# First loads of a two-layer decoder kernel: small tables issued ahead of the input, over two DMA queues

## The chip, the cores and the metric

The kernel runs on one core of one Trainium2 chip. The metric is the device time of one execution in microseconds (us), from its first to its last instruction with what the launch adds around it; lower is better. The kernel before takes 354.22 us (median of three runs).

## The reference, cut to what matters

A decoder of two layers works on an input `x` of 256 positions by 1024 features, all in float32. The first layer is an RWKV-7 time mixing, the second a block-sparse attention. What matters here is only how the first layer begins:

```
h  = x * rsqrt(mean(x*x) + 1e-6) * norm_a          # RMS norm, one row per position
xx = shift_by_one_position(h) - h
out_i = (h + xx * mu[i]) @ w_in[:, columns of i]    # i = 0..5: r, decay, k, v, rate, gate
```

`norm_a` is one vector of 1024 numbers, `mu` six of them, `w_in` a 1024 x 4224 matrix. Everything else in the two layers comes after these products.

## The kernel before, in words

The 256 positions are two blocks b of 128 (the partitions of a tile) and the 1024 features two halves n of 512, so x is four tiles of 128 x 512, called here x(n,b): `xb[n, b]`, 256 KB each. They are loaded by four DMAs on the queue of SyncE (SP).

For one block, `norm_row(b)` (line 689) lets ScalarE (ACT) square the two halves and sum each (tile `sq`, lines 691 to 693), VectorE (DVE) add the two sums (tile `rs`, line 695) and GpSimd (POOL) take the power -0.5 (`rsqrt`, line 524). `block(b)` (line 721) then waits for the event "vT" and starts `normed(b, q, r)` (line 699) for both halves q: DVE multiplies x by the row's factor (tile `xn`, line 704), TensorE (PE) transposes it by an identity matrix (line 706), and the transposed tile is multiplied by `norm_a` on its way from PSUM into `hT` (on DVE for q = 0, line 708; on ACT for q = 1, line 712). DVE then forms the difference `xxT` (line 718). From hT and xxT come the mixed inputs `u`, their high and low parts `zhi` and `zlo`, and the first matrix products.

The vectors `norm_a` (8 rows of 128) and `mu` (48 rows of 128) are loaded as one tile `vrow` of 56 rows, transposed by PE (`start`, line 739, and `columns`, line 727) and copied by DVE into `vT`, so that each feature's factor lies on its partition. The identity is the first 128 columns of the table `con`, 64 KB in 128 rows of 512 bytes.

The order of the work on each engine is not written by hand. The kernel is a set of generators; a small planner in Python, the class `Weave` (line 100), walks through them at build time with an estimated cost for every operation, and emits the instructions of each engine in the order in which its own clock reaches them. An engine then runs its instructions strictly in that order on the chip. DMAs are a lane "D" of the planner (`dma`, line 422); all of them go to SP's queue. The first ones are issued by `fetch` (line 495) with the most urgent priority of the loads at the start, -3, in this order: x(0,0), x(1,0), identity, norm weights, mu, x(0,1), x(1,1), two loads of `wl` (the narrow columns of `w_in`), and then the first weight quarter `raw`.

`warm_up` (line 1626) fills PE from the start with matrix products on a tile of zeros, `ps<-zero` in the profile, until the planner's clock says 9.16; they stand in PE's fixed order between the transposes of the start. ACT begins with a table load and one activation `warm` (line 489) that needs that table.

The helper at line 308 records all of DVE's, ACT's and POOL's operations, line 424 the DMAs, line 413 the matrix products and line 417 the transposes, so in the rows these are told apart by their tiles.

Of the kernel before, what the change touches and what calls it, by code (L numbers as in the profile page):

```python
# [12 lines left out]
AF = mybir.ActivationFunctionType  # L13
# [3 lines left out]
P = 128  # L17
T = 256
NB = 2
D = 1024  # L20
# [79 lines left out]
class Weave:  # L100
# [18 lines left out]
    def spawn(self, gen, prio):  # L119

        end, last, fresh = Event(), [None], [0.0]
        self.parts += 1

        def resume(value=None, waited=False):
            if waited:
                fresh[0] = self.now + LAT
            while True:
                try:
                    w = gen.send(value)
                except StopIteration:  # L130
                    self.parts -= 1
                    self.fire(end)
                    return
                value = None
                if isinstance(w, (Op, list)):
                    ops = [w] if isinstance(w, Op) else w
                    left = [len(ops)]

                    def through(op):
                        left[0] -= 1  # L140
                        if not left[0]:
                            last[0] = op.eng if len(ops) == 1 else None
                            resume()
                    for op in ops:
                        self.submit(op, prio, last[0], fresh[0], through)
                    if ops:
                        return
                elif isinstance(w, Event):
                    if w.done is None:
                        w.waiters.append(resume)  # L150
                        return
                    fresh[0] = max(fresh[0], w.done + LAT)
                elif isinstance(w, (Slots, tuple)):
                    slots, n = w if isinstance(w, tuple) else (w, 0)
                    if len(slots.places) < max(n, 1) or slots.waiters and (not slots.urgent or slots.waiters[0][0] <= prio):
                        slots.wait(prio, resume, n)
                        return
                    fresh[0] = max(fresh[0], slots.since + LAT)
                    value = slots.take(n)
                else:  # L160
                    self.at(self.now + w, resume)
                    return
        self.at(self.now, resume)
        return end
# [196 lines left out]
def yoco(ctx, tc, consts, x, norm_a, mu_a, w_in_a, w0_a, w2_a, a0_a, a2_a, kk_a, ka_a, rk_a,  # L361
         gn_w_a, gn_b_a, w_out_a, norm_kv, w_kv, k_norm, norm_b, w_in_b, q_norm_b, w_out_b, out):
    nc = tc.nc
    x2, out2 = x[0], out[0]
# [9 lines left out]
    spawn = weave.spawn  # L374
# [7 lines left out]
    def T_(tag, name, shape=(P, 512), dt=F32):  # L382

        return up.tile(list(shape), dt, name=nm(name), tag=tag, bufs=1)

    def keep(shape, name):
        return cp.tile(list(shape), F32, name=nm(name))
# [34 lines left out]
    def dma(*pairs):  # L422
        us = sum(max(0.475, math.prod(a.shape) * 4 / 260e3 * (2 if a.shape[-1] < 128 else 1)) for a, _ in pairs)
        return Op("D", us, lambda: [nc.sync.dma_start(a, b) for a, b in pairs])
# [43 lines left out]
    def hs(n):  # L468
        return slice(n * 512, (n + 1) * 512)
# [9 lines left out]
    def event(key):  # L479
        return ev.setdefault(key, Event())  # L480

    def fire(key):
        weave.fire(event(key))


    half = keep((P, 8), "half")
    nc.gpsimd.memset(half, -0.5)
    warm = keep((P, 1), "warm")
    nc.scalar.activation(warm, half[:, 0:1], AF.Tanh)
    con = keep((P, C_TRI), "con")  # L490
    xb = {(n, b): T_(f"kk{n}{b}", "x") for n, b in HB}
    vrow, vrow2 = T_("tmp", "vrow", (56, P)), T_("z1", "vrow", (16, P))
    wl = T_("ab", "wl", (P, KT, 2, 64))

    def fetch(key, *pairs):
        yield dma(*pairs)
        fire(key)

    def fetch_first(b):
        for n in range(2):  # L500
            spawn(fetch(f"x{n}{b}", (xb[n, b], x2[b * P:(b + 1) * P, hs(n)])), -3)
    fetch_first(0)
    spawn(fetch("ident", (con[:, 0:128], consts[0:P, 0:128])), -3)
    spawn(fetch("vrow", (vrow[0:8], norm_a[0].rearrange("(a p) -> a p", p=P)),
                (vrow[8:56], mu_a[0].rearrange("i (a p) -> (i a) p", p=P))), -3)
    fetch_first(1)
    spawn(fetch("wl", *((wl[:, :, i, :], w_in_a[0, :, c:c + 64].rearrange("(a p) f -> p a f", p=P))
                        for i, c in enumerate((1024, 3136)))), -3)
# [8 lines left out]
    ident = con[:, C_ID:C_ID + 128]  # L517
# [843 lines left out]
    for i, label in enumerate(ORDER_A):  # L1361
        key, n = label[0], int(label[1])
# [242 lines left out]
    for i, label in enumerate(ORDER_B):  # L1605
        key, n = label[0], int(label[1])
# [152 lines left out]
```

## Time and profile before

| what | value |
|---|---|
| time, median of 3 runs (lowest to highest) | 354.22 us (353.51 to 354.46) |
| the profiled execution's own time | 354.56 us |
| its span, first to last instruction | 352.7 us |
| PE busy | 342.2 us, 97% of the span |
| DVE busy | 286.6 us, 81% |
| ACT busy | 211.1 us, 60% |
| DMA moved | 51.44 MB, mean 146 GB/s |
| mean granted TensorE clock | 0.995 of full speed |

The span is what one profiled execution shows, instruction by instruction; the time of the same execution lies 1.86 us above it. Shares are means over the whole span: the start, of which the change is a part, is some 20 us of it and has limits of its own. A row of a timeline gives the start, the length, the engine, the line, the operation and the tiles, written before and read after the arrow, and in brackets how long the engine had been idle and who ended that.

### The profile page before, as it was taken

To read this page: it belongs to the slowest core of one execution; us is meant where nothing else is said; L and a number is where in the kernel's file an instruction comes from. 1 tells how busy PE (TensorE), PEld (TensorE's weight loads), DVE (VectorE), ACT (ScalarE), POOL (GpSimd) and SP (SyncE) were. 2 spreads that over 40 slices of the span, in tenths; PEclk is the share of its full clock that TensorE was granted. 3 is DMA by queue.
4 is the path that set the end of the run, shared out by engine and by line. 5 is a ranking of instruction groups with operands and counts; after the bars stand their busy time and mean duration, and the time that the engine had idled before them with its cause. 6 is when DMAs were issued, how large, how long until landed. Compare 5 with 4: busy or idle time off the path is not lost.

```text
span 352.7 us, 7611 instructions
## 1 busy us (share of the span) xinstructions
PE 342.2 (97%) x3006; PEld 266.1 (75%) x3006; DVE 286.6 (81%) x572; ACT 211.1 (60%) x415; POOL 46.7 (13%) x71
## 2 busy tenths in 40 slices
PE   8798999999999999999999999999999999999995
PEld 8774877778466775568777788788888878889784
DVE  2899789999999869959769989648868987769823
ACT  5379986754247852265673556645578775688620
POOL 1200050000310000200220522005504005000000
PEclk9899999999999999999999999999999999999999
DMA  7674762673254912356535512565540266503603
GB/s 197 179 205 137 240 192 77 171 215 94 89 151 125 239 59 61 91 134 233 189 111 180 187 60 73 198 222 185 175 164 2 77 228 223 190 1 122 205 35 119
DMA packets 29740, 51.44 MB, mean 146 GB/s; under 512 B 4412, under 2 KB 5764, under 8 KB 29704
## 3 DMA queue, kind: packets, MB, share of 16 engines
q1 hardware_dynamic: 29704, 50.94, 47.4%
q8 instruction: 24, 0.39, 0.5%
q14 instruction: 12, 0.10, 0.1%
HBM read 48.31 MB, written 1.05 MB: 140 GB/s over the span
## 4 chain that ended last, share of the span: by engine, by line
PE 82%; DVE 13%; DMA 1%; issue 1%; POOL 0%; ACT 0%; SPq 0%; DVEq 0%
PE acc L413 56%; PE ps L413 19%; PE ps L417 6%; DVE u L308 3%; DVE wlo L308 2%; DVE zlo L308 1%; DMA tri<-in_consts_dram 1%; DVE z L308 1%; DVE k L308 1%; DVE x L308 1%; DVE xxT L308 1%; DVE tmp L308 1%; DVE kkh L308 1%; DVE XF L308 0%; POOL rs L308 0%
## 5 line engine op out<-in xcount | busy, mean ns | idle before, releaser
L308 DVE TENSOR_TENSOR wlo<-raw,whi 128x1024 fp32r<-128x1024 f32 x70 | 85.4, 1222 | 25.2 <-ACT whi L308 25.0
L308 ACT ACTIVATE whi<-raw 128x1024 fp32r<-128x1024 f32 x70 | 74.1, 1064 | 39.4 <-PE acc L413 23.7
L413 PE MATMUL acc<-wlo,zhi 128*128 128x512 f32 x120 | 51.6, 430 | 1.0 <-DVE wlo L308 1.0
L413 PE MATMUL acc<-whi,zlo 128*128 128x512 f32 x120 | 47.1, 393 | 0.6 <-DVE zlo L308 0.6
L413 PE MATMUL acc<-whi,zhi 128*128 128x512 f32 x120 | 47.1, 392 | 0.0
L413 PE MATMUL acc<-whi,z 128*128 128x512 f32 x128 | 39.8, 392 | 0.0
L413 PEld LDWEIGHTS acc<-wlo,zhi 128*128 128x128 f32 x120 | 22.5, 188 | 7.3 <-DVE wlo L308 1.4
L413 PEld LDWEIGHTS acc<-whi,z 128*128 128x128 f32 x128 | 24.1, 188 | 4.9
L413 PEld LDWEIGHTS acc<-whi,zhi 128*128 128x128 f32 x120 | 22.5, 188 | 5.0
L413 PEld LDWEIGHTS acc<-whi,zlo 128*128 128x128 f32 x120 | 22.6, 189 | 4.8 <-DVE zlo L308 0.9
L413 PE MATMUL acc<-wlo,z 128*128 128x512 f32 x64 | 26.0, 406 | 0.0
L413 PE MATMUL acc<-zb,whi 128*128 128x256 f32 x128 | 23.3, 282 | 0.0
L413 PE MATMUL acc<-whi,zb 128*128 128x512 f32 x64 | 20.0, 394 | 0.0
L413 PE MATMUL acc<-whi,zf 128*128 128x512 f32 x64 | 19.8, 390 | 0.0
L413 PEld LDWEIGHTS acc<-zb,whi 128*128 128x128 f32 x128 | 19.7, 189 | 0.1
L413 PE MATMUL acc<-zb,wlo 128*128 128x256 f32 x64 | 18.9, 295 | 0.0
L308 POOL TENSOR_TENSOR nrm<-nrm,half 128x8 f32<-128x8 f32 x4 | 8.1, 2021 | 78.0 <-DVE nrm L308 78.0
L413 PE MATMUL acc<-raw,zlo 128*128 128x512 f32 x32 | 15.5, 605 | 0.0
L413 PE MATMUL acc<-raw,zhi 128*128 128x512 f32 x32 | 15.0, 606 | 0.0
L413 PEld LDWEIGHTS acc<-wlo,z 128*128 128x128 f32 x64 | 12.1, 189 | 2.9 <-issue 0.5
L413 PEld LDWEIGHTS acc<-whi,zb 128*128 128x128 f32 x64 | 12.1, 189 | 2.6
L308 ACT ACTIVATE zhi<-u 128x256 fp32r<-128x256 f32 (+1 forms) x16 | 7.9, 522 | 10.1 <-DVE u L308 7.0
(215 smaller groups left out, 721.6 us busy)
## 6 DMA issues: line engine op xcount, KB each, us to landing
raw<-in_w_in_a_dram SPq DMA_DIRECT2D x32, 512.0 KB, 4.3
raw<-in_w_kv_dram SPq DMA_DIRECT2D x16, 512.0 KB, 3.7
raw<-in_w_in_b_dram SPq DMA_DIRECT2D x16, 512.0 KB, 4.2
raw<-in_w_out_a_dram SPq DMA_DIRECT2D x8, 512.0 KB, 4.9
raw<-in_w_out_b_dram SPq DMA_DIRECT2D x8, 512.0 KB, 4.5
x<-in_x_dram SPq DMA_DIRECT2D x8, 256.0 KB, 4.4
out_dram<-x SPq DMA_DIRECT2D x8, 128.0 KB, 1.9
NBK<-kkh SPq DMA_DIRECT2D x6, 128.0 KB, 5.8
```

The lines of the kernel that those rows point to most:

```text
L308: op = Op(eng, us, lambda: getattr(obj, name)(*a, **k), table=table, banks=banks(*a, *k.values()), port=port(eng, name, us, a, k))
L413: return us, lambda: nc.tensor.matmul(dst, l, r, **kw), size(r) * (1 if l.dtype == F32R else 4) * min(l.shape[0], size(l)) / P, banks(dst) ...
L417: return max(0.045, 0.1085 * src.shape[0] / P), lambda: nc.tensor.transpose(dst, src, idt), 256 * src.shape[0] / P, banks(dst), src.shape[ ...
```

## The change

The loads of mu, of the norm weights and of the identity are written out ahead of the planner's work. Mu goes to SP's queue as its first DMA; the norm weights, the identity and the tile x(1,0) go, in that order, to ACT's own queue, ahead of the activation `warm`. The other three tiles of x stay on SP's queue, behind mu. In the planner the load of x(1,0) keeps its place and its cost and emits nothing, and one empty operation of the lane D, with the cost of the three small loads (0.475 us each), takes the place of these and then fires both of their events; so the planner's clock, and with it the order of all other instructions, is meant to stay as it was.

```diff
     half = keep((P, 8), "half")
     nc.gpsimd.memset(half, -0.5)
     warm = keep((P, 1), "warm")
-    nc.scalar.activation(warm, half[:, 0:1], AF.Tanh)
     con = keep((P, C_TRI), "con")
     xb = {(n, b): T_(f"kk{n}{b}", "x") for n, b in HB}
     vrow, vrow2 = T_("tmp", "vrow", (56, P)), T_("z1", "vrow", (16, P))
     wl = T_("ab", "wl", (P, KT, 2, 64))
 
-    def fetch(key, *pairs):
-        yield dma(*pairs)
+
+    nc.sync.dma_start(vrow[8:56], mu_a[0].rearrange("i (a p) -> (i a) p", p=P))
+    for a, b in ((vrow[0:8], norm_a[0].rearrange("(a p) -> a p", p=P)), (con[:, 0:128], consts[0:P, 0:128]),
+                 (xb[1, 0], x2[0:P, 512:1024])):
+        nc.scalar.dma_start(a, b)
+    nc.scalar.activation(warm, half[:, 0:1], AF.Tanh)
+
+    def fetch(key, *pairs, issued=False):
+        op = dma(*pairs)
+        if issued:
+            op.emit = lambda: None
+        yield op
         fire(key)
 
     def fetch_first(b):
         for n in range(2):
-            spawn(fetch(f"x{n}{b}", (xb[n, b], x2[b * P:(b + 1) * P, hs(n)])), -3)
+            spawn(fetch(f"x{n}{b}", (xb[n, b], x2[b * P:(b + 1) * P, hs(n)]), issued=(n, b) == (1, 0)), -3)
     fetch_first(0)
-    spawn(fetch("ident", (con[:, 0:128], consts[0:P, 0:128])), -3)
-    spawn(fetch("vrow", (vrow[0:8], norm_a[0].rearrange("(a p) -> a p", p=P)),
-                (vrow[8:56], mu_a[0].rearrange("i (a p) -> (i a) p", p=P))), -3)
+    def small():
+        yield Op("D", 0.475 * 3, lambda: None)
+        fire("ident")
+        fire("vrow")
+    spawn(small(), -3)
     fetch_first(1)
```

## Rows read from the trace of the kernel before

**Rows 1.** The page: its span and the busy time of TensorE.

```profile
span 352.7 us, 7611 instructions
PE 342.2 (97%) x3006; PEld 266.1 (75%) x3006; DVE 286.6 (81%) x572; ACT 211.1 (60%) x415; POOL 46.7 (13%) x71
```

**Rows 2.** The chain that ended last, 0 to 40 us: start, length, what.

```profile
1.04 4.82 PE ps L413 x22
...
6.06 1.09 PE ps L413 x8
...
7.62 0.70 DVE hT L308
...
11.87 4.31 PE ps L413 x24
```

**Rows 3.** Timeline of SP's queue, the first DMA issues.

```profile
0.72 0.86 SPq L424 DMA_DIRECT2D x<-in_x_dram  x2
1.63 0.42 SPq L424 DMA_DIRECT2D con<-in_consts_dram  x1
2.09 0.38 SPq L424 DMA_DIRECT2D vrow<-in_norm_a_dram  x1
2.51 0.32 SPq L424 DMA_DIRECT2D vrow<-in_mu_a_dram  x1
2.87 0.90 SPq L424 DMA_DIRECT2D x<-in_x_dram  x2
```

**Rows 4.** Timeline of ACT, 0 to 8 us.

```profile
0.72 1.28 ACT L489 ACT_TABLE_LOAD   x1 [0.72 <-PEq L1748]
2.01 0.20 ACT L489 ACTIVATE warm<-half 128x1 f32<-128x1 f32 x1
3.39 0.63 ACT L308 ACTIVATE sq<-x 128x512 f32<-128x512 f32 x1 [1.18 <-DMA x<-in_x_dram]
...
4.25 0.63 ACT L308 ACTIVATE sq<-x 128x512 f32<-128x512 f32 x1
...
6.37 0.63 ACT L308 ACTIVATE sq<-x 128x512 f32<-128x512 f32 x1 [1.39 <-DMA x<-in_x_dram]
...
7.07 0.63 ACT L308 ACTIVATE sq<-x 128x512 f32<-128x512 f32 x1
```

**Rows 5.** Timeline of DVE, 5 to 12 us.

```profile
5.01 0.16 DVE L308 TENSOR_TENSOR rs<-ssq 128x1 f32<-128x1 f32 x1 [4.03 <-ACT sq L308]
6.09 0.22 DVE L308 COPY vT<-ps 128x56 f32<-128x56 f32 x1 [0.93 <-PE ps L417]
6.23 0.87 DVE L308 TENSOR_SCALAR xn<-x,rs 128x512 f32<-128x512 f32 x2
...
8.96 0.15 DVE L308 TENSOR_TENSOR rs<-ssq 128x1 f32<-128x1 f32 x1
...
10.48 1.14 DVE L308 TENSOR_SCALAR xn<-x,rs 128x512 f32<-128x512 f32 x2
```

**Rows 6.** Timeline of POOL, the power of block 0.

```profile
5.53 0.58 POOL L308 TENSOR_TENSOR rs<-rs,half 128x1 f32<-128x1 f32 x1
```

**Rows 7.** Timeline of PE, the transposes of the start.

```profile
5.79 0.27 PE L417 MATMUL ps<-con,vrow 56*128 56x56 f32 x1
...
6.98 1.04 PE L417 MATMUL ps<-con,xn 128*128 128x128 f32 x8
...
11.24 0.63 PE L417 MATMUL ps<-con,xn 128*128 128x128 f32 x4 [2.11 <-DVE xn L308]
```

**Rows 8.** Busy time by stretch; the last three columns: granted clock, DMA share, GB/s.

```profile
2.00:2.65 0.65, 0.65 (x5) 0.65 (x4) 0.00 (x0) 0.20 (x1) 0.00 (x0) 1.00 0.99 369
2.65:3.40 0.75, 0.75 (x6) 0.75 (x5) 0.00 (x0) 0.01 (x1) 0.00 (x0) 1.00 1.01 327
3.40:4.25 0.85, 0.85 (x6) 0.85 (x6) 0.00 (x0) 0.71 (x2) 0.00 (x0) 1.00 0.69 162
...
12.32:15.73 3.41, 3.41 (x18) 3.41 (x18) 3.41 (x7) 0.42 (x1) 0.00 (x0) 0.50 0.42 155
```

## The prediction

> **What bounds the kernel now.** I began with the page: PE is busy for 342.2 of 352.7 us [rows 1], so a change that touches only loads can pay only where PE's stream waits for them, and that is the start. So I went next to the chain that ended last, cut to the first 40 us. The reader should see that no DMA stands in its first 16 us: it goes through 22 warm-up products, eight more warm-ups, DVE's hT, and, from 11.87, 24 narrow products of PE [rows 2]. The loads that the change moves lie beside this chain, and the question is how close to it they are. Three timelines tell that.
>
> x of block 0: ACT's second square starts at 4.25 [rows 4], DVE's sum follows at 5.01, POOL's power ends at 6.11 [rows 6], and the first xn starts at 6.23 [rows 5]. Its first half ends about 0.44 later, half of 0.87, at 6.67; the transposes stand at 6.98 [rows 7]. How long such a handover takes is shown by block 1: its first xn starts at 10.48 and, with half of 1.14, ends at 11.05, and PE, which had been idle, starts at 11.24 [rows 5, 7]: 0.19 us. So in block 0 the transposes could have started at 6.86; they stood behind the eight warm-ups, and **x of block 0 has about 0.1 us to spare**, no more.
>
> mu, norm weights, identity: their transpose stands at 5.79 [rows 7], right where the 22 warm-ups, of 4.82 us from 1.04, end [rows 2]. The warm-ups are in PE's fixed order, so these tables would not be used earlier if they landed earlier.
>
> x of block 1: its squares start at 6.37 and 7.07 and the second ends at 7.70 [rows 4]. DVE's sum of them is at 8.96 [rows 5], because it stands behind hT and xxT of block 0 in DVE's order: over 1 us to spare.
>
> **The change part by part.** The sum is made against the profiled execution: 354.56 us, of which 352.7 are its span and 1.86 lie around it. The median of the runs, 354.22, is 0.34 lower, and the change of the span is added to that.
>
> 1. SP loses three issues ahead of x(0,1): the identity, 0.42, the norm weights, 0.38, and x(1,0), half of 0.86 [rows 3]. Mu, 0.32, moves to the front. x(0,1), issued at 2.87 before, comes at 0.72 + 0.32 + 0.43 and two gaps of 0.04, about 1.55; it, x(1,1), wl and raw are issued some 1.3 us earlier. Worth: **0**, since the sum of block 1's squares stands behind DVE's work on block 0 (above), and so does all that uses wl and raw. The cover would be gone only if hT came over 1 us earlier, and step 2 excludes that.
>
> 2. The small tables land earlier. Worth: **0**. A gain would need the warm-ups to be shorter. At most it is the 0.1 us by which the transposes of block 0 stand behind the warm-ups, and that only if x came earlier as well.
>
> 3. ACT gets three issues ahead of its table load. The trace has no issue from ACT; the nearest rows are SP's, 0.32 to 0.43 each [rows 3]. With 0.42 each, ACT's table load (1.28) and `warm` (0.20) [rows 4] end at 0.72 + 3 x 0.42 + 1.48 = 3.46, 0.07 after the first square before (3.39). As x lands later too (step 4), this is covered: **0**. The cover ends at issues of about 0.6 us: then ACT would be free at 4.0.
>
> 4. x(0,0) and x(1,0) are issued later: x(0,0) behind mu, 1.08 for 0.72, x(1,0) behind two issues on ACT, 0.72 + 0.38 + 0.42 + 0.08 = 1.60 for about 1.15: later by 0.45. And the 94 KB of small tables, in rows of 512 bytes, now move ahead of x or beside it. The stretches show what that means: from 2.00 to 3.40 the queues moved 240 and 245 KB at 369 and 327 GB/s, nearly the 524 KB of the two tiles, and they were full (share 0.99 and 1.01); then came the small tables, and the pace fell to 162 GB/s [rows 8]. 94 KB at that pace are 0.58 us. The lower end for x(1,0)'s delay is 0.1, if the small tables fill time in which nothing else is ready to move (before 2.00) and ACT issues faster than SP; the upper end, with both queues issuing side by side, is 0.95: 0.58, and 0.37 more if half of x(1,0), 131 KB, has to share the pace of about 350 with as many bytes of x(0,1). I take **0.6**, near the 0.58, since the rows show the queues full at this time, so that bytes set ahead of x delay it by what they take.
>
> Here the Trainium skill speaks against the change ("DMA: Bandwidth & Descriptors", section "Queues, rings and completion order"): each DMA engine goes round between the queues that have work, one packet at a time. By that x(1,0) on ACT's queue shares with x(0,1) on SP's, and the sum would take the upper end, 0.95. No row here has two queues, so the trace doesn't decide it.
>
> 5. What the 0.6 does: second square at 4.85, power's end at 6.71, xn at 6.83. vT is no longer what DVE does just before. The transposes follow 0.6 - 0.1 = 0.5 later, hT at about 8.1. From 7.62 on DVE and then PE run nearly without a gap, each row of block 1 standing behind block 0 in DVE's order [rows 2, 5], so that the 0.5 is handed on, to PE's first transposes of block 1 at about 11.75 and from there to the whole stream. Nothing in the rows takes it up again; the bounds are 0 and 0.85.
>
> Sum: 0 + 0 + 0 + 0.5. A profiled execution of 355.1 (span 353.2), and a median of **354.7 us**, 0.14% over 354.22. A measurement of this kernel tells differences of about 0.3% from no change, that is 1.06 us, so the forecast is: **no change that can be measured**, leaning to slower.
>
> **The rivals.** *Slower: the two queues issue in turn.* If an issue holds something that SP and ACT share, they take turns: mu 0.32, norm 0.38, x(0,0) 0.43, identity 0.42, x(0,1) 0.43, with five gaps of 0.04, and x(1,0) is issued at 0.72 + 1.98 + 0.20 = 2.90 in place of 1.15, 1.75 later. Its landing moves by as much, ACT's square starts at about 6.0, and the chain pays 1.65: 355.9 us, 0.47% slower. It decides as soon as the second square starts after 5.4 (4.25 + 0.1 + 1.06). For it: six issues now compete in the first 2 us. Against it: the issues on SP differ by shape only from 0.32 to 0.43 [rows 3], which looks like work of the issuing engine itself. The Trainium skill ("Perfetto Trace Analysis", section "DMA Instruction — HWDGE (DVE, Sync)") says that such an issue takes a lock on a descriptor generator which the sequencers share, which is this rival's mechanism; no row here shows two engines issuing. Chance 0.2.
>
> *Nothing lands later.* The small tables fit into the time before x's data flow and x(1,0) gains on its own queue what it loses in issue time. Then block 0 stays behind its warm-ups, block 1 behind DVE's order, and the time is 354.2. For it: 1.28 us pass between the first issue, 0.72, and full pace at 2.00 [rows 3, 8]. Against it: the full queues from 2.00 on. Chance 0.22; the verdict is the same as the forecast's.
>
> *Faster: the clock doesn't fall.* From 12.32 to 15.73 the granted clock is 0.50 of full speed, the lower of TensorE's two levels, after PE had been idle for 2.11 us ahead of 11.24 [rows 7, 8]. Those 3.41 us do the work of 1.7 at full clock. If the shift of the start lets PE's activity fall so that the clock stays up, up to 1.7 us come back, less the 0.5: 353.0 us. Against it: block 1's transposes wait for xn, which stands in DVE's order behind block 0's work, so both edges of the idle time move by the same 0.5 and it stays as long; and DVE is busy for all of 12.32 to 15.73 as well [rows 8], so that a faster PE would gain less than 1.7. Chance 0.08.
>
> *The change isn't what it says.* If the empty operation in the planner shifted its clock, the order would change everywhere, in either direction. It takes 3 x 0.475, the same as the loads it stands for, and both events are waited for together in `start`, so I give it 0.05, split evenly.
>
> **How the numbers follow.** The forecast (x later by 0.1 to 0.95 us) has 0.45, and the rivals 0.2, 0.22, 0.08 and 0.05. Slower by over 0.3%: 0.2 for the queues in turn, 0.03 of the last rival, and 0.02 from the forecast's upper end: 0.25. Faster: 0.08 and 0.03: 0.11. The rest, 0.64, is the same. The likeliest case gives 354.7. The range runs from 353.5, the lowest run of before, which the case of no delay can show again, to 356.0, just past the queues in turn; outside it are the clock and the changed order.
>
> **What would show it.** Right: in the changed profile ACT's second square starts at 4.7 to 5.2, the transposes of block 0 at 7.3 to 7.7, block 1's at 11.5 to 12, with vT still at about 6.1 and the clock's fall still there; x(0,1)'s square is earlier and DVE's sum for block 1 is still behind xxT. Step 3 would be wrong if `warm` ended after 4.0, step 4 if the second square started before 4.3 or after 5.4, step 5 if the transposes of block 1 came at the old 11.24 although those of block 0 are late, or if the delay is gone by 40 us. A clock of 1.00 between 12.3 and 15.7 would mean the faster rival.

## The result, and the profile after

The changed kernel takes **357.04 us** (median of six runs, 356.05 to 361.45); the kernel before, run beside it, takes 354.18 (353.51 to 355.46). The ratio is 1.0072, with a 95% interval of 1.0048 to 1.0097: slower, by 2.86 us in the medians and 2.56 in the means that the ratio compares. Medians in this text are over all runs of a kernel, while the ratios leave out runs more than 1.5% above the fastest of the same kernel. The profiled execution took 357.46 us, 2.90 more than that of before (354.56).

First the page. The span grew from 352.7 to 355.6 us and PE's busy time only from 342.2 to 342.6 [rows 1], so 2.5 of the 2.9 us lost are time in which PE had nothing to do:

```profile
span 355.6 us, 7611 instructions
...
PE 342.6 (96%) x3006; PEld 266.2 (75%) x3006; DVE 286.3 (81%) x572; ACT 210.8 (59%) x415; POOL 46.9 (13%) x71
...
q10 hardware_dynamic: 304, 0.33, 0.3%
```

SP's queue is q1 in such lines, ACT's q10, which carries 0.33 MB: the norm weights, the identity and x(1,0).

Then the chain that ended last, cut to its first 12 us (start, length, what). In [rows 2] no DMA stood in it. Now it begins with ACT's three issues and, from the last of them on, 5.56 us until x has landed:

```profile
1.75 5.56 DMA x<-in_x_dram
7.34 0.73 ACT sq L308 x2
...
9.23 0.50 DVE xn L308
9.78 0.67 PE ps L417 x4
10.47 0.70 DVE hT L308
```

Which x that is, the timelines of SP's queue and of ACT say (columns as in [rows 3, 4]):

```profile
0.72 0.39 SPq L495 DMA_DIRECT2D vrow<-in_mu_a_dram  x1
1.17 1.36 SPq L424 DMA_DIRECT2D x<-in_x_dram  x3
...
0.72 0.60 ACTq L498 DMA_DIRECT2D vrow<-in_norm_a_dram  x1
1.35 0.37 ACTq L498 DMA_DIRECT2D con<-in_consts_dram  x1
1.75 0.44 ACTq L498 DMA_DIRECT2D x<-in_x_dram  x1
...
3.52 0.20 ACT L499 ACTIVATE warm<-half 128x1 f32<-128x1 f32 x1
4.41 0.63 ACT L308 ACTIVATE sq<-x 128x512 f32<-128x512 f32 x1 [0.69 <-DMA x<-in_x_dram]
...
7.34 0.63 ACT L308 ACTIVATE sq<-x 128x512 f32<-128x512 f32 x1 [2.21 <-DMA x<-in_x_dram]
...
7.96 0.61 ACT L308 ACTIVATE sq<-x 128x512 f32<-128x512 f32 x1
```

The square of x(0,0) starts at 4.41 in place of 3.39, that of x(1,0), which came over ACT's queue, at **7.34 in place of 4.25** [rows 4]. The first square of block 1 follows without a wait at 7.96, and the second behind it: their tiles were there, but ACT's order keeps them behind the late one.

How the 3.09 us are handed on is read from DVE and PE (the number before an arrow is idle time):

```profile
8.09 0.16 DVE L308 TENSOR_TENSOR rs<-ssq 128x1 f32<-128x1 f32 x1 [7.11 <-ACT sq L308]
8.17 0.21 DVE L308 COPY vT<-ps 128x56 f32<-128x56 f32 x1
...
9.78 1.09 PE L417 MATMUL ps<-con,xn 128*128 128x128 f32 x8 [3.19 <-DVE xn L308]
...
14.10 1.08 PE L417 MATMUL ps<-con,xn 128*128 128x128 f32 x4 [1.43 <-DVE xn L308]
...
24.07 0.23 PE L417 MATMUL ps<-con,vrow 16*128 16x16 f32 x1
```

Against [rows 2, 5, 7]: block 0's transposes +2.80 (9.78 for 6.98), hT +2.85 (10.47 for 7.62), block 1's first transposes +2.86 (14.10 for 11.24). The 16-row transposes at 24.07, and ACT's later table loads, stand in the timelines of before at

```profile
21.01 0.23 PE L417 MATMUL ps<-con,vrow 16*128 16x16 f32 x1
...
24.35 1.28 ACT L308 ACT_TABLE_LOAD   x1
...
325.61 1.28 ACT L308 ACT_TABLE_LOAD   x1
```

and the table loads in that of after at

```profile
27.42 1.28 ACT L308 ACT_TABLE_LOAD   x1
...
328.52 1.28 ACT L308 ACT_TABLE_LOAD   x1
```

that is +3.06, +3.07 and, 300 us on, +2.91. What is lost by 14 us is still lost at the end.

The clock falls in after as well, and for longer (stretches of after, columns as in [rows 8]; the third number from the right is the granted clock):

```profile
12.30:15.70 3.40, 1.97 (x10) 1.71 (x10) 3.40 (x8) 1.36 (x2) 1.75 (x4) 0.50 0.19 74
15.70:18.00 2.30, 2.30 (x13) 2.30 (x13) 2.30 (x6) 0.42 (x1) 0.00 (x0) 0.51 0.00 0
```

In before the low level, 0.50, ended at 15.73 [rows 8]; here it reaches to 18. But from block 1's transposes to the 16-row ones it takes 24.07 - 14.10 = 9.97 us here and 21.01 - 11.24 = 9.77 in before, so the longer fall costs 0.2 us, and the late x the rest.

Last, what the queues moved, in three stretches of after of 1 us each, from 4, 5 and 6 us (packets, MB, share of the 16 engines' time):

```profile
q1 hardware_dynamic: 105, 0.19, 65.0%
q10 hardware_dynamic: 73, 0.09, 32.1%
...
q1 hardware_dynamic: 121, 0.17, 49.1%
q10 hardware_dynamic: 96, 0.17, 48.5%
...
q1 hardware_dynamic: 798, 0.29, 109.1%
q10 hardware_dynamic: 10, 0.02, 4.3%
```

x(1,0), issued at 1.75, moves mostly between 4 and 6, at a third to a half of the engines' time, beside x(0,1) and x(1,1). Its last eight rows of 2 KB, with two packets of 4 bytes, come only between 6 and 7, among 798 packets of SP's queue, most of them short rows of `wl`. The tile is complete with the last of them; whether `wl` held them up is asked in e6.

### The profile page after: what moved, and what is told of

Read it like the earlier page. It is cut to its first block, busy times and chain, and to the rows that moved or that the text cites. A ratio compares the mean times of both kernels' runs of the same rounds, so it can differ in the third digit from the quotient of the medians.

```text
span 355.6 us, 7611 instructions
## 1 busy us (share of the span) xinstructions
PE 342.6 (96%) x3006; PEld 266.2 (75%) x3006; DVE 286.3 (81%) x572; ACT 210.8 (59%) x415; POOL 46.9 (13%) x71
## 4 chain that ended last, share of the span: by engine, by line
PE 80%; DVE 14%; DMA 2%; issue 2%; POOL 1%; ACT 1%; ACTq 0%; DVEq 0%
PE acc L413 56%; PE ps L413 17%; PE ps L417 6%; DVE u L308 4%; DVE zlo L308 2%; DVE wlo L308 2%; DMA x<-in_x_dram 2%; DVE z L308 1%; POOL rs L308 1%; DVE x L308 1%; DVE xxT L308 1%; DVE tmp L308 1%; DVE k L308 1%; DVE kkh L308 1%; DVE XF L308 0%
## 5 line engine op out<-in xcount | busy, mean ns | idle before, releaser
L308 POOL TENSOR_SCALAR vr<-vr 128x8 f32<-128x8 f32 x4 | 2.3, 563 | 91.2 <-DVE vr L308 91.2
```

The lines of the kernel that those rows point to most:

```text
L308: op = Op(eng, us, lambda: getattr(obj, name)(*a, **k), table=table, banks=banks(*a, *k.values()), port=port(eng, name, us, a, k))
```

## The experiments

None of the kernels below computes anything else than the reference; where products on zeros are added, their results are used by nothing.

**e1: the tables alone.** As the change, but x(1,0) stays on SP's queue:

```diff
-    for a, b in ((vrow[0:8], norm_a[0].rearrange("(a p) -> a p", p=P)), (con[:, 0:128], consts[0:P, 0:128]),
-                 (xb[1, 0], x2[0:P, 512:1024])):
+    for a, b in ((vrow[0:8], norm_a[0].rearrange("(a p) -> a p", p=P)), (con[:, 0:128], consts[0:P, 0:128]),):
...
-            spawn(fetch(f"x{n}{b}", (xb[n, b], x2[b * P:(b + 1) * P, hs(n)]), issued=(n, b) == (1, 0)), -3)
+            spawn(fetch(f"x{n}{b}", (xb[n, b], x2[b * P:(b + 1) * P, hs(n)]), issued=False), -3)
```

> Edit: the small tables go ahead as in the change (mu first on SP, norm weights and identity on ACT's queue), but x(1,0) stays on SP's queue, right behind x(0,0). Theory 1 (x(1,0) is late because it stands on a queue of its own, on which it takes turns with all that SP has queued): with x(1,0) back in SP's line the second square starts at 4.6 to 5.3 in place of 7.34, and the time is 354.2 to 355.0. Theory 2 (the bytes and issues of the small tables set ahead of x cost it): the second square starts after 6.3 and the time stays above 356.0.

Measured: 355.76 us (12 runs) beside 354.78 of before; ratio 1.0018 (0.9992 to 1.0044). ACT's squares in the profile:

```profile
4.42 0.63 ACT L308 ACTIVATE sq<-x 128x512 f32<-128x512 f32 x1 [1.17 <-DMA x<-in_x_dram]
...
5.22 0.63 ACT L308 ACTIVATE sq<-x 128x512 f32<-128x512 f32 x1
```

The first square is as late as in the change (4.42 and 4.41), the second 0.97 later than before and not 3.09; block 1's transposes are at 11.97, +0.73. The second square is in the band that I gave for theory 1, the time 0.76 us above its band. So the tables ahead of x cost about 1 us at the squares, and the other 2.1 come with x(1,0) on ACT's queue. Taken at one mean clock, 1.000, the runs say the same: 354.02 (5 runs) against 353.11 of before (4), 0.9 us.

**e2: x(1,0) alone.** Before, with x(1,0) as the first and only DMA of ACT; the tables keep their places on SP's queue, and the planner's load of x(1,0) emits nothing:

```diff
...
+    for a, b in ((xb[1, 0], x2[0:P, 512:1024]),):
+        nc.scalar.dma_start(a, b)
+    nc.scalar.activation(warm, half[:, 0:1], AF.Tanh)
...
```

> Edit: only x(1,0) moves, as the one DMA on ACT's queue, issued at the very start; identity, norm weights and mu stay on SP behind x(0,0). Theory 1 (a queue of its own, in turns with SP's line): x(1,0) shares with x(0,0), the tables and x(0,1); the second square starts at 4.8 or later, though it is issued 0.4 us earlier than before, and the time is 354.7 to 356.5. Theory 2 (the tables ahead of x): nothing stands ahead, the second square starts at 4.0 to 4.3 and the time is within 0.3 us of before.

Measured: 355.75 us, ratio 1.0037 (1.0007 to 1.0068): slower, as theory 1 had it. The profiled execution took 362.17 us, with a clock of 0.50 to 0.60 from 165 to 175; only its start is read here. The squares start at 4.26 and 4.89, back to back: x(0,0) lands 0.87 later than alone, x(1,0) no later than 4.89, so that the second square is 0.64 later than before. Block 1's transposes are at 11.62, +0.38. Here x(1,0) is issued at 0.72, beside x(0,0) and ahead of all else, and nothing like the change's 7.34 appears. A second queue costs something by itself, but not the 3.09 us; what stands ahead of x(1,0) on it, and what runs beside it meanwhile, has to make the rest.

**e3: the change, with SP held.** Behind x(0,0), SP issues a copy of 32 bytes of x(1,0), which must wait for its landing; all later loads of SP's queue wait behind that:

```diff
...
     def small():
-        yield Op("D", 0.475 * 3, lambda: None)
+        yield Op("D", 0.475 * 3, lambda: nc.sync.dma_start(held, xb[1, 0][0:1, 0:8]))
```

> Edit: the change, with one more DMA on SP's queue ahead of x(0,1) that copies 32 bytes out of x(1,0), so that SP issues x(0,1), x(1,1), wl and raw only once x(1,0) has landed. Theory 1 (x(1,0) is held up by what SP has queued behind x(0,0)): the competition is gone, the second square starts at 4.4 to 5.2 in place of 7.34, block 0 is as early as that; block 1 comes later for lack of x(0,1), which lands at about 8.5, so the time is between 354.5 and 356.5. Theory 2 (tables ahead of x): the second square stays after 6.3 and the time rises above 358.

Measured: 358.56 us (9 runs), ratio 1.0079 (1.0047 to 1.0112). ACT's squares:

```profile
4.39 0.63 ACT L308 ACTIVATE sq<-x 128x512 f32<-128x512 f32 x1 [0.70 <-DMA x<-in_x_dram]
5.11 0.63 ACT L308 ACTIVATE sq<-x 128x512 f32<-128x512 f32 x1
9.14 0.63 ACT L308 ACTIVATE sq<-x 128x512 f32<-128x512 f32 x1 [3.31 <-DMA x<-in_x_dram]
```

and the packets of ACT's queue in the stretches 3 to 4, 4 to 4.5 and 4.5 to 5.5 us:

```profile
q10 hardware_dynamic: 224, 0.24, 71.9%
...
q10 hardware_dynamic: 61, 0.09, 46.9%
...
q10 hardware_dynamic: 3, 0.00, 1.1%
```

This is the run that decides. With the same issues on ACT at the same times, but nothing behind x(0,0) on SP's queue, the second square starts at 5.11, 0.09 us behind the end of the first. SP's copy, which waits for the same tile, is issued at 5.11 as well, so that is when x(1,0) had landed, and not only when ACT came free. **The 2.23 us between 5.11 and 7.34 are the price of SP's backlog** (1.3 to 2.3 in the four executions with the change's loads, as the second square starts between 6.43 and 7.38 in them). The rest, 5.11 - 4.25 = 0.86, is close to the 0.97 that e1 found for the tables. The time I had expected to fall with it (354.5 to 356.5) didn't: the hold moves the lateness to block 1, whose first square is at 9.14 and whose transposes are at 13.44.

**e4: x(1,0) first on ACT's queue**, the tables behind it:

```diff
-    for a, b in ((vrow[0:8], norm_a[0].rearrange("(a p) -> a p", p=P)), (con[:, 0:128], consts[0:P, 0:128]),
-                 (xb[1, 0], x2[0:P, 512:1024])):
+    for a, b in ((xb[1, 0], x2[0:P, 512:1024]), (vrow[0:8], norm_a[0].rearrange("(a p) -> a p", p=P)), (con[:, 0:128], consts[0:P, 0:128]),):
```

> Edit: the change with another order on ACT's queue: x(1,0) first, then norm weights and identity. Theory 1 (in turns with SP's line): x(1,0) starts early and has only mu, x(0,0) and x(0,1) to share with: the second square starts at 4.3 to 5.5 and the time is 354.3 to 355.5. Theory 2 (tables ahead of x): the second square starts at 4.1 to 4.4, the time is that of before. Should it still start after 6.5, then neither the tables nor its place in ACT's line matter, but ACT's queue itself.

Measured: 355.23 us, ratio 1.0012 (0.9986 to 1.0038). The squares are at 4.71 and 5.34, back to back, so x(1,0) is no longer waited for. The identity is, now the last on ACT's queue, and PE waits for it:

```profile
7.18 0.32 PE L417 MATMUL ps<-con,vrow 56*128 56x56 f32 x1 [1.08 <-DMA con<-in_consts_dram]
```

So x(1,0) isn't late for any property of its own: with this order it is the identity, last on ACT's queue while SP's is full, that comes late. In this execution block 1's transposes are at 14.07, as late as in the change, and it took 355.54 us with a clock of 0.997; the runs as a whole aren't shown to be slower than before. Whether the identity comes earlier in the others, or the delay is made up later, no run tells.

**e5: the change once more**, beside the runs of before that e6 to e8 share.

> Edit: none; the changed kernel once more, on the chip of the runs beside it and timed as often. If the late x(1,0) explains the loss, executions with the same granted clock differ by 2.2 to 3.0 us between the two kernels, the second square starts between 6.8 and 7.6 whatever the clock does, and the medians differ by 2 to 4 us. Rival, that the loss is mostly a clock that falls more often: executions with the same granted clock differ by less than 1 us.

Measured: 356.97 us (12 runs, 354.12 to 359.06) beside 355.64 (35 runs); ratio 1.0045 (1.0006 to 1.0084). In this execution the second square is at

```profile
6.51 0.63 ACT L308 ACTIVATE sq<-x 128x512 f32<-128x512 f32 x1 [1.49 <-DMA x<-in_x_dram]
```

and block 1's transposes are at 13.26: the same delay, 2.26 instead of 3.09 us, below what I expected. At a mean clock of 0.995 the runs are 356.96 (9) against 355.54 (14), +1.4, which is neither the 2.2 to 3.0 that I gave for the late x nor the rival's less than 1; at 1.000 one run, 354.12, against 353.25 (6). How late x(1,0) is differs from execution to execution. That the loss follows it isn't shown: the ratios of the two comparisons, 1.0045 and 1.0072, have intervals that overlap.

**e6: only `wl` and `raw` held.** The copy of e3 stands ahead of `wl`, so x(0,1) and x(1,1) still run beside x(1,0):

```diff
...
+        if key == "wl":
+            op.emit = lambda: [nc.sync.dma_start(held, xb[1, 0][0:1, 0:8])] + [nc.sync.dma_start(a, b) for a, b in pairs]
...
```

> Edit: the change, with 32 bytes copied out of x(1,0) on SP's queue between x(1,1) and wl, so that only wl and raw wait for x(1,0), and x(0,1) and x(1,1) stand beside it as in the change. If the rows of wl, 256 bytes each, hold up the last packets of x(1,0), the second square starts at 5.9 to 6.5 in place of 7.34. If sharing with x(0,1) and x(1,1) does it all, it starts after 6.9. If neither, before 5.6. The time is between that of the change less 1 us and the change.

Measured: 358.00 us, ratio 1.0053 (1.0005 to 1.0100). The time is above the change's in these rounds (356.97), where I had expected it below. The second square:

```profile
6.41 0.63 ACT L308 ACTIVATE sq<-x 128x512 f32<-128x512 f32 x1 [1.36 <-DMA x<-in_x_dram]
```

It is in the expected band; but e5, without the hold, had 6.51. From e3 to here, 1.30 us (5.11 to 6.41, one execution each) are due to x(0,1) and x(1,1). What `wl` and `raw` add would be 0.1 by e5's execution and 0.93 by the first one's.

The starts of the single packets in the traces tell more. In e5 and e9 the last row of x(1,0) starts at 6.06 and 5.96, ahead of the first row of `wl` (6.24 and 6.17): there `wl` and `raw` had no part. In the first execution of the change and in e12 the last rows of x(1,0), eight and four of them, follow each other at about 0.16 us in two series and in one, with a 2 KB row of SP's queue in between, which is x(0,1)'s or x(1,1)'s; in e3, with SP held, the last ones follow at 0.08. So in the late executions, too, it is with x that these rows take turns and not with the 256-byte rows of `wl`. Why a few rows come so late in two of four executions stays open.

**e7: all of x first on SP's queue, the three tables on ACT's.** Against before, with the change's empty operation in the planner for the three tables:

```diff
+    for a, b in ((vrow[0:8], norm_a[0].rearrange("(a p) -> a p", p=P)), (vrow[8:56], mu_a[0].rearrange("i (a p) -> (i a) p", p=P)),
+                 (con[:, 0:128], consts[0:P, 0:128])):
+        nc.scalar.dma_start(a, b)
+    nc.scalar.activation(warm, half[:, 0:1], AF.Tanh)
...
```

> Edit: all four tiles of x on SP's queue in the old order, first; norm weights, mu and identity on ACT's queue. If what stands on ACT's queue is served in turn with SP's line, x(0,0) lands as before or up to 0.4 us later (first square 3.4 to 3.8), x(1,0) at 4.3 to 5.0, and the identity, the last on ACT's queue, lands late, as the last of a queue does beside wl: the transpose of the tables starts at 5.8 to 7.2. Time 0 to 1.2 us above before. If the small tables cost x only because they stood ahead, both squares start as before and so does the transpose, and the time is that of before within 0.3 us.

Measured: 355.49 us beside 355.64, ratio 0.9984 (0.9948 to 1.0019): no difference. The first square stands right behind `warm`, at 3.56, the second at 4.88, later than before (4.25). The transpose of the tables is at 6.16 for 5.79, but the 22 warm-ups ahead of it end at 6.10 for 5.86, so at most 0.13 us of that are the tables'. Block 1's transposes are at 11.86. x isn't free of the tables on the second queue either; the order of before is as good.

**e8: before, with eight more warm-ups** behind block 0's transposes, to take the clock's fall away. PE would be idle there [rows 7].

```diff
             yield pe(mm(t[:, 0:P], z, z, 0.2155, start=True, stop=True))
+        for _ in range(8):
+            nc.tensor.matmul(t[:, 0:P], z, z, start=True, stop=True)
```

> Edit: the kernel before, with eight more warm-up products on PE behind those that end at 9.1, in the idle time ahead of block 1's transposes (2.11 us); no load is touched. Theory on the clock: the granted clock falls in most executions because of this idle time, and a fall costs about 1.8 us. Then the mean granted clock is 1.000 in nearly all executions and the median is 1.2 to 2.0 us below before (352.8 to 353.5). Rival: the falls have another cause, or DVE is what ends this stretch anyway; then executions with a clock of 0.995 stay as frequent, or the time stays within 0.5 us.

Measured: 353.94 us beside 355.64; ratio 0.9978 (0.9947 to 1.0009). The mean clock is 0.998 to 1.000 in all 12 runs, where before had 0.995 in 14 of 35 and less in 12. In the profile the 16-row transposes come at 19.45 for 21.01, and ACT's table loads are 1.49 early at 22.86, 0.63 early at 127.95 and 0.26 late at 260.29: part of the gain is given back, among others in an "issue" wait of 0.7 us of PE that the waits of before don't list. A gain isn't shown: the interval takes in 1, and the runs that the ratio compares have medians of 353.94 and 354.21.

**e9: the change with such warm-ups.** Ten behind the transpose of the tables and eight at the end:

```diff
...
+            made += 1
+            if made == 15:
+                for _ in range(10):
+                    nc.tensor.matmul(t[:, 0:P], z, z, start=True, stop=True)
+        for _ in range(8):
+            nc.tensor.matmul(t[:, 0:P], z, z, start=True, stop=True)
```

> Edit: the change, with ten more warm-up products ahead of block 0's transposes and eight behind them, so that PE's two idle times at the start are filled and the clock has no cause to fall there. If the loss is x's late arrival, the clock stays at 1.000 and the time lies 1.2 to 2.6 us above the kernel before with its own eight more warm-ups (353.9 in the run before, so 355.1 to 356.5). Rival, that the change loses only by a clock that falls more often: 353.4 to 354.4, that of the other within 0.5 us.

Measured: 361.87 us (6 runs) beside 355.15; ratio 1.0133 (1.0031 to 1.0235). At the start the clock stays up, and the 16-row transposes come at 21.32, +1.87 against e8's 19.45 with a second square at 6.43. But later PE waits twice for its own instructions, and the clock falls there. PE's longest wait and one stretch:

```profile
PE ps L413 <- issue: 3.3, 2, 1.7
```

```profile
110.00:115.00 5.00, 5.00 (x68) 3.18 (x58) 4.40 (x7) 1.95 (x6) 0.00 (x0) 0.66 0.59 161
```

Waits at these places stand in other runs too (last section); the time of e9 says nothing of the late x. It led to e11 and e12, which add no instruction to PE.

**e10: e8 once more**, beside e9.

> Edit: the kernel before with eight more warm-up products ahead of block 1's transposes, once more. If they hold the clock up, the mean granted clock is 0.998 to 1.000 in all executions again, and the median is 1 to 2 us below that of before in the same rounds (353.3 to 354.2). If the gain of the run before was chance, the medians are within 0.7 us.

Measured: 354.39 us beside 355.15, ratio 0.9987 (0.9950 to 1.0024). The interval takes in 1, and the runs that it compares have the same median, 354.39. The clock was 0.994 or 0.995 in three of the 12 runs, so the eight products don't always hold it up; I had expected that they would.

**e11 and e12: wider warm-ups, as many instructions.** In before the last of the warm-ups become 320 columns wide in place of 128; in the change four become 448 and the rest 320 wide:

```diff
...
+            if made >= 15:
+                op.emit = lambda: nc.tensor.matmul(t[:, 0:320], z, wide, start=True, stop=True)
...
+            if made >= 11:
+                op.emit = lambda n=448 if made < 15 else 320: nc.tensor.matmul(t[:, 0:n], z, wide[:, 0:n], start=True, stop=True)
```

> Edit: the kernel before, with the five warm-up products behind block 0's transposes made 320 columns wide in place of 128, so that they fill some 1.6 us of the idle time ahead of block 1's transposes while the number of PE's instructions stays; no load is touched. If the clock falls because of that idle time, and the eight added products of the earlier run gave some of their gain back by shifting PE's later instructions, then the clock is 0.998 to 1.000 in nearly all executions and the median is 1.2 to 2.2 us below before, in the same rounds, and in its profile the gain at 24 us is still there at 260 us. If the added products' shift had no part in it, this does no better than they did (0.7 to 1.7 us).

> Edit: the change, with the four warm-up products ahead of block 0's transposes 448 columns wide and the five behind them 320, so that both idle times of PE at the start are filled with the same number of instructions. This holds the clock in both kernels and leaves the price of the late x alone: if that is what the change loses, the time lies 1.5 to 2.8 us above the kernel before with its wide warm-ups, with a clock of 0.998 to 1.000. If the change loses mostly by a clock that falls more often, the two lie within 0.7 us of each other.

Measured: e11 356.20 us, ratio 1.0011 (0.9969 to 1.0053); e12 358.75, ratio 1.0082 (1.0045 to 1.0119); both beside 355.32 of before. The start of e11, and then that of e12, on PE:

```profile
11.02 0.63 PE L417 MATMUL ps<-con,xn 128*128 128x128 f32 x4 [0.53 <-DVE xn L308]
...
19.17 0.23 PE L417 MATMUL ps<-con,vrow 16*128 16x16 f32 x1
```

```profile
14.13 0.63 PE L417 MATMUL ps<-con,xn 128*128 128x128 f32 x4 [0.53 <-DVE xn L308]
...
22.27 0.23 PE L417 MATMUL ps<-con,vrow 16*128 16x16 f32 x1
```

Between the two marks there are 8.15 us in e11 and 8.14 in e12: full clock in both, and the late x, whose square starts at 7.38 here, costs 14.13 - 11.02 = 3.11 us, still 3.10 at the second mark. **The loss doesn't need the clock.** In runs with a mean clock of 0.998 and more the medians are 353.36 (e11, 4 runs, 352.87 to 353.75) and 356.18 (e12, 5 runs, 354.76 to 358.36), 2.8 apart. I had expected the clock to stay up in nearly all runs, and it didn't (0.998 or more in 4 and in 5 of 12): in e11's profile it is up at the start and falls later, after PE had waited 1.51 us for its own instructions ahead of 160.80:

```profile
160.00:170.00 10.00, 9.20 (x155) 7.95 (x156) 4.91 (x10) 5.77 (x12) 0.00 (x0) 0.58 0.38 132
```

## Why the prediction was wrong

The forecast was 354.7 us, inside what a measurement can't tell from no change; it became 357.04, above the range. In sign the forecast leaned the right way, and the place was right; the size was not.

**Step 1 (worth 0): right in worth, wrong in what it said of ACT.** x(0,1) and x(1,1) were issued earlier, by 2.53 in place of 3.77 [rows 3], and wl and raw with them, but x(0,1)'s square didn't come earlier. It starts at 7.96 for 6.37, since ACT's fixed order puts it behind the square of x(1,0). And the earlier issues were not free: x(0,1) and x(1,1) are the backlog that x(1,0) had to share with. I had counted them as loads without a user in a hurry, and not as traffic.

**Step 2 (the tables land earlier, worth 0): right.** PE took up the tables at 5.23 for 5.79, behind its warm-ups as before, which took 4.26 us for 4.82 in this execution; nothing came of it.

**Step 3 (ACT's issues, worth 0): right.** They took 0.60, 0.37 and 0.44 for the 0.42 each that I assumed; `warm` ended at 3.72 for the 3.46 of the sum, ahead of the first x at 4.41 (4.0 was the bound).

**Step 4 failed, at "I take 0.6" and at its upper end, 0.95.** The second square is 3.09 later. By second squares the parts are these: 4.25 before; 5.22 in e1 and 5.11 in e3, about 0.9 for the tables ahead of x; 6.41 in e6, 1.3 for x(0,1) and x(1,1) on SP's queue; 6.43 to 7.38 in four executions with the change's loads, of which two have up to 0.97 more, in rows of x(1,0) that come late beside x and not beside wl (e6). Why they do is open. The step had the first part at 0.58, taking the bytes and leaving out the 0.45 by which x is issued later; the two together would have been 1.03, close to e1's 0.97, though no run separates them. The second part it put at 0.37, half of x(1,0) sharing with as many bytes of one tile; it measured 1.3 to 2.3. That x(1,0), the last of its queue and behind the identity, would share with both tiles of block 1 for nearly all of its rows, I didn't work out.

The rule of the Trainium skill that stood against the change ("DMA: Bandwidth & Descriptors", "Queues, rings and completion order") says that a DMA engine goes round between the queues with work, packet by packet. By it I should have taken the upper end. The trace agrees: from 5 to 6 us the two queues moved 0.17 MB each, and the last rows of x(1,0) take turns with rows of SP's queue (e6). The rule alone doesn't give the size: the upper end that I had tied to it was 0.95, and the delay 3.09.

**Step 5 (nothing takes it up): right, but for the slack.** 2.85 at hT, 2.86 at block 1, 2.91 at 328 us. The slack ahead of block 0's transposes was 0.29 us (3.09 - 2.80) and not 0.1: the first xn starts 3.00 later, since vT is no longer ahead of it, and PE 0.55 behind that start for the 0.75 of before, where I had counted 0.63 as needed (0.44 and 0.19). Behind them nothing more is taken up. vT, which I had left at 6.1, went with the square, at 8.17 for 6.09, since DVE has it behind the sum `rs`.

**The rival "the two queues issue in turn" came nearest in time, 355.9, and isn't what happened.** Its mark, a second square after 5.4, was reached for another reason: ACT issued x(1,0) at 1.75, not at 2.90, beside SP's issues (0.39, then three in 1.36), and e3 with the same issues has the square at 5.11. The lock that "Perfetto Trace Analysis", section "DMA Instruction — HWDGE (DVE, Sync)" of the Trainium skill, describes doesn't show in these rows as a cost of this size: the norm weights took 0.60 on ACT for 0.38 on SP, for a reason that no run settles, but e2's x(1,0), issued at 0.72 like SP's x(0,0), took 0.42.

**The rival "the clock doesn't fall" failed too.** It fell for longer, at 0.2 us of cost in the profiled execution. The idle time didn't stay as long, as I had argued, but moved: 3.19 us ahead of block 0's transposes and 1.43 ahead of block 1's, for 2.11 ahead of the latter alone [rows 7]. "Nothing lands later" is excluded by the squares, and "the change isn't what it says" by the order of all other instructions on the engines, which stayed.

No kernel of these runs is shown to be faster than before: the ratios of e8 and e10 have intervals that take in 1.

## What to carry to other kernels

One queue in order was a protection here: on SP's queue x(1,0) was used at 4.25, ahead of all that was issued behind it, and on a second queue it shared the engines with the two tiles issued on the first, up to its last row (6.43 to 7.38). Before moving a load to another queue, list what will be in flight beside it until it lands, and not only what stands ahead of it; move a load that has slack, or hold the other queue back, and see that the hold isn't paid by the next user. Where the slack is small, as here the 0.29 us ahead of block 0's transposes, nearly all of a load's delay is paid (2.80 of 3.09 us).

## What the runs showed of the hardware that I had not expected

The clock's fall at the start isn't a property of the kernel. I read it from one execution as if it were. In the profiles of e1 and e7 PE idles for the same 2.11 us ahead of block 1's transposes as in that of before, and the clock stays at 1.00 there. Among the 32 runs of before beside e1 to e4 the mean granted clock was 1.000 in four (median 353.11 us), 0.995 in eighteen (354.94), and 0.984 to 0.986 in five (358.08 to 359.52). The step from the first to the second, 1.83 us, is near what one low stretch costs: block 1's start took 9.77 us in the profile of before, with the fall, and 8.15 in e11's, without, 1.62 less.

PE waits for its own instructions near 107 and 162 us, and for how long differs: 0.9 us at most in before, but 1.7 and 1.6 in e9, 1.5 in e11 and 1.6 in e12. I took the added products on zeros for the cause, and the other runs don't bear that out: e2, which has none, waits for 1.2 and 2.1 us at these places, e3 and e6 for 1.3 at the later one, and e8 and e10, which have eight, for 0.9 at most. Behind the later wait the clock fell in e11 (0.58 from 160 to 170), e9, e2 and e6, and not in e3 and e12. Why the waits come is open.

How late x(1,0) lands differs in the same program: the second square started at 7.34 and 6.51 in two executions of the change, at 6.43 in e9 and 7.38 in e12, which have the same loads. With the loads of before it differs less: 4.25, 4.49, 4.16 and 4.28 in before, e8, e10 and e11.
